# A fused decoder block on one core: attention operands stored contiguously in DRAM, queries held in half tiles

## The chip, the core and the metric

The kernel runs on one core of a Trainium2 chip, in one launch. The metric is the device time of one execution in microseconds; smaller is better. Inputs and outputs are float32.

## What is computed

One decoder layer on a sequence of 2048 tokens of width 1024, then a final norm. Cut to what matters here:

```python
h = rmsnorm(x, norm1_g)
p = h @ w_in                       # 2560 columns: pooling, q/k/v of two attentions
a = pool_mixer(p[..., :256])
b = diff_attention(...)            # 4 heads, two 64-wide softmax maps, 128-wide values
c = stick_breaking_attention(...)  # 4 heads of 64
x = x + concat(a, b, c) @ w_out
x = x + (silu(h2 @ w_gate) * (h2 @ w_up)) @ w_down     # h2 = rmsnorm(x, norm2_g)
return rmsnorm(x, final_norm_g)
# scores, both kinds: q (scaled by 1/8) . k over 64 channels, causal
```

## The kernel before

**Tiling.** The sequence is cut in `NT` = 4 tiles of `TQ` = 512 tokens. `a1_tile` (L534) does one tile of the first part: norm, transposes (`norm_transpose`, L453 to L469), and the projection in ten units of 256 columns (`UNITS[t]`, L37). `attention` (L838) goes over the same tiles and, in `ORDER[t]` (L36), over six pairs of heads: four of the differential attention (`att_diff`, L710), two of stick-breaking attention (`att_sb`, L789). Then come `out_proj` and `mlp`, which the change does not touch.

**Precision.** Matmul operands are split in a high and a low float32r part (`split`, L414: ScalarE casts at L415, VectorE subtracts at L416). Dense products take three matmuls (`mm3`, L473 to L476). A score takes two, and packs the parts in the partitions: a key tile holds the 64 channels of the high part in partitions 0 to 63 and of the low part in 64 to 127; the query operand holds the same 64 channels twice, `q[0]` with the high part, `q[1]` with the low one. So L657 gives q_high times (k_high + k_low) and L658 adds q_low times the same. L660 adds the causal mask.

**Through DRAM.** Projected queries and keys come out as 128 rows (two heads or maps `r` of 64 channels) by 512 tokens. They are split into a buffer `st` (L601 and L603 for queries), stored to `q_d` or `k_d` (L611, one store of 512 KB, high and low parts as two planes of all 2048 tokens), and loaded in the other arrangement: `load_q` (L622) makes four loads of 256 KB for a pair and tile (L626: two parts, each twice, into 64 partitions), `load_kv` (L632) two of 256 KB for a key tile (L635) and one of 512 KB or two of 256 KB for values (L640, L645). Before the scores of query tile t, a pair needs its queries of tile t and its keys and values of tiles 0 to t.

**Buffers.** SBUF is laid out in rings of slots. `q0` and `q1` have the slots w31 and w32, and a second one each, w12 and w13, which come free only when the projections' ring `wr` (same slots) has served its last weight. Keys have four slots, two more later; so do values. A slot is loaded again when its last reader is done.

**Order.** All operations are recorded with an engine, an estimated duration, buffers and a priority. `Plan.schedule` (L145) lays them out on five engines by its own estimates (`dma_ns`, `LAG`, `MORE`), and the result is the fixed order of every engine's instructions. Projections of tiles 1 to 3 have lower priority on TensorE than attention: they fill what attention leaves. All loads and stores are issued by SP, in order: one that waits for a buffer or for data holds back those behind it.

Of the kernel before, what the change touches and what calls it, by code (L numbers as in the profile page):

```python
# [19 lines left out]
P = 128  # L20
S = 2048
# [26 lines left out]
def f32(ap):  # L48
    return ap.bitcast(F32)
# [226 lines left out]
def hybrid_block_kernel(  # L276
# [24 lines left out]
    q_d = [dram.tile([2, P, S], F32, name=f"q_d{p}") for p in range(PAIRS)]  # L301
    k_d = [dram.tile([2, P, S], F32, name=f"k_d{p}") for p in range(PAIRS)]
    vd_d = [dram.tile([P, S // P, 2, P], F32, name=f"vd_d{p}") for p in range(DIFF_PAIRS)]
    vs_d = [dram.tile([P, S // P, 2, 64], F32, name=f"vs_d{p}") for p in range(2 * SB_PAIRS)]
# [229 lines left out]
    def a1_tile(pl, rg, t, prio, prio_pe, first):  # L534
# [10 lines left out]
        if t == 0:  # L545
            constants(pl, {"w": rb["q1"], "h": rb["p0"]}, prio + 0.5, xs[3:])
        late = []
        for un in UNITS[t]:
# [30 lines left out]
            for c, ps in enumerate(pend):  # L579
# [4 lines left out]
                if is_v:  # L584
# [3 lines left out]
                    for h in range(nh):  # L588
                        split(pl, lambda h=h, stv=stv: stv()[:, h, :, 0, :], lambda h=h, stv=stv: stv()[:, h, :, 1, :],
                              lambda h=h, pv=pv: pv()[:, :, h, :], TQ // nh, True, [ps], (st, (h, 0)), (st, (h, 1)),  # L590
                              prio)
                        dst = vs_d[h] if un == 9 else vd_d[2 * (un - 5) + h]
                        pr = DIFF_PAIRS + h // 2 if un == 9 else 2 * (un - 5) + h
                        blk0 = 4 * t + 2 * c
                        pl.op("dma", dma_ns(P * 4096 // nh), lambda dst=dst, blk0=blk0, h=h, stv=stv: nc.sync.dma_start(
                            dst[:, blk0:blk0 + 2, :, :], f32(stv()[:, h])), r=[(st, (h, 0)), (st, (h, 1))],
                            w=[(m_v[pr][t], (c, h))], prio=prio)
                else:
                    isq = un in (1, 2, 7)
                    if isq:  # L600
                        pl.op("act", act_ns(TQ), lambda st=st, ps=ps: nc.scalar.mul(st.t[:, 0, :], ps.t, 0.125),  # L601
                              r=[ps], w=[(st, 0)], prio=prio)
                        pl.op("dve", dve_ns(TQ), lambda st=st, ps=ps: nc.vector.scalar_tensor_tensor(  # L603
                            st.t[:, 1, :], ps.t, 0.125, f32(st.t[:, 0, :]), ALU.mult, ALU.subtract),
                            r=[ps, (st, 0)], w=[(st, 1)], prio=prio)
                    else:
                        split(pl, lambda st=st: st.t[:, 0, :], lambda st=st: st.t[:, 1, :], lambda ps=ps: ps.t,
                              TQ, True, [ps], (st, 0), (st, 1), prio)
                    pair = {1: 0, 2: 2, 7: 4, 3: 0, 4: 2, 8: 4}[un] + c
                    dst, mk = (q_d, m_q) if isq else (k_d, m_k)  # L610
                    pl.op("dma", dma_ns(P * 4096), lambda st=st, dst=dst[pair]: nc.sync.dma_start(  # L611
                        dst[:, :, t0:t0 + TQ].rearrange("l p t -> p l t"), f32(st.t)),
                        r=[st], w=[mk[pair][t]], prio=prio)
# [8 lines left out]
    def load_q(pl, rg, t, p, prio):  # L622
        q = [rg["q0"].new(), rg["q1"].new()]
        for hl in range(2):
            for dup in range(2):
                pl.op("dma", dma_ns(64 * 4096) * 1.3, lambda hl=hl, dup=dup: nc.sync.dma_start(  # L626
                    f32(q[hl].t[64 * dup:64 * dup + 64]),
                    q_d[p][hl, :, t * TQ:(t + 1) * TQ].rearrange("(r d) t -> d r t", r=2)),
                    r=[m_q[p][t]], w=[(q[hl], dup)], prio=prio)
        return q  # L630

    def load_kv(pl, rg, p, j, prio):  # L632
        k, v = rg["k"].new(), rg["v"].new()
        for hl in range(2):
            pl.op("dma", dma_ns(64 * 4096) * 1.3, lambda hl=hl: nc.sync.dma_start(  # L635
                f32(k.t[64 * hl:64 * hl + 64]),
                k_d[p][hl, :, j * TQ:(j + 1) * TQ].rearrange("(r d) t -> d r t", r=2)),
                r=[m_k[p][j]], w=[(k, hl)], prio=prio)
        if p < DIFF_PAIRS:
            pl.op("dma", dma_ns(P * 4096), lambda: nc.sync.dma_start(  # L640
                f32(v.t), vd_d[p][:, 4 * j:4 * j + 4].rearrange("p b l e -> p (b l e)")),
                r=[m_v[p][j]], w=[v], prio=prio)
        else:
            for r in range(2):
                pl.op("dma", dma_ns(P * 2048), lambda r=r: nc.sync.dma_start(  # L645
                    f32(v.t[:, r * TQ:(r + 1) * TQ]),
                    vs_d[2 * (p - DIFF_PAIRS) + r][:, 4 * j:4 * j + 4].rearrange("p b l e -> p (b l e)")),
                    r=[m_v[p][j]], w=[(v, r)], prio=prio)
        return k, v

    def scores(pl, rg, q, kt, r, g, j, t, strict, prio):
        n = TQ if j < t else (g + 1) * P
        s = rg["s"].new()
        qs = slice(g * P, (g + 1) * P)

        def qk():
            nc.tensor.matmul(s.t[:, :n], q[0].t[:, r, qs], kt.t[:, r, :n], start=True, stop=False)  # L657
            nc.tensor.matmul(s.t[:, :n], q[1].t[:, r, qs], kt.t[:, r, :n], start=False, stop=j < t)  # L658
# [3 lines left out]
        pl.op("pe", 2 * mm_ns(n) + (60 if j == t else 0), qk, r=[*q, kt], w=[s], prio=prio)  # L662
# [713 lines left out]
    def banks(ids):  # L1376
# [22 lines left out]
        q0=ring([2, TQ], F32R, ("w", [31, 12])), q1=ring([2, TQ], F32R, ("w", [32, 13])),  # L1399
# [73 lines left out]
```

## Time and profile before

| what | value |
|---|---|
| median of three runs | 2718.97 us (2711.99 to 2724.35) |
| the profiled execution | 2719.03 us, its span 2717.2 us |
| PE (TensorE matmul) busy | 2601.9 us, 96% |
| DVE, ACT, POOL busy | 1786.2 us, 1319.3 us, 870.0 us |
| share of the chain that ended last | PE 72%, DMA 9%, DVE 9% |
| loads of q_d, k_d | 96 and 120, of 256 KB |
| stores to q_d, k_d | 24 and 24, of 512 KB |

The profile is of one execution. Busy time of TensorE is the union of matmuls that overlap in its pipeline: one of 512 columns shows about 0.4 us, but the next begins 0.23 us after it. "[1.27 <-DMA d<-q_d]" behind an instruction says that its engine stood idle for 1.27 us, ended by a transfer from `q_d`. All tiles in SBUF are called `d`; lines tell them apart. [...] The first 1390 us hold projections, attention and output projection; the rest is the MLP.

### The profile page before, as it was taken

What the parts mean: (1) busy time and instruction counts of PE and PEld (TensorE: products, weight loads), DVE (VectorE), ACT (ScalarE), POOL (GpSimd) and SP (SyncE); (2) the same over time, 40 slices, a digit from 0 to 9 for tenths busy, and PEclk for the clock granted to TensorE, in tenths of its full rate; (3) what the DMA queues carried; (4) which work ended last, traced back from release to release, by engine and by line L of the source; (5) the groups of instructions that cost most, each with busy time, mean ns of one, the idle gap of its engine ahead of it and who ended that gap; (6) DMA issues with size and microseconds to landing.
All of it is one profiled execution on the core that took longest, in us unless ns stands there. A gap on an engine that the chain in (4) does not pass through costs nothing.

```text
span 2717.2 us, 39503 instructions
## 1 busy us (share of the span) xinstructions
PE 2601.9 (96%) x13836; PEld 2176.7 (80%) x13836; DVE 1786.2 (66%) x3131; ACT 1319.3 (49%) x2645; POOL 870.0 (32%) x890
## 2 busy tenths in 40 slices
PE   9989989989999999999989999999999998999998
PEld 7878778877888788888978877888888886888886
DVE  6366787758887888788656666545444447558557
ACT  4365566646666666665534444323333333445444
POOL 1001212212254124133015456535454544132041
PEclk9989999989999999999999999999999999999999
DMA  6786585556564775664534457465222338335223
GB/s 217 245 251 184 160 245 160 155 155 202 153 177 147 225 203 147 192 178 161 166 118 155 155 184 239 158 220 199 101 102 97 109 129 291 118 95 194 93 90 120
DMA packets 223480, 454.27 MB, mean 167 GB/s; under 512 B 23720, under 2 KB 70952, under 8 KB 223280
## 3 DMA queue, kind: packets, MB, share of 16 engines
q1 hardware_dynamic: 223280, 451.75, 52.9%
q8 instruction: 108, 1.77, 0.3%
q14 instruction: 92, 0.75, 0.1%
HBM read 321.11 MB, written 130.55 MB: 166 GB/s over the span
## 4 chain that ended last, share of the span: by engine, by line
PE 72%; DMA 9%; DVE 9%; issue 3%; ACT 2%; POOL 1%; SPq 1%; DVEq 0%; ACTq 0%; POOLq 0%
PE bank L474 16%; PE bank L476 16%; PE bank L475 16%; DVE d L416 4%; DMA d<-q_d 4%; PE bank L657 3%; PE bank L681 3%; PE bank L658 3%; DMA d<-wo_d 2%; PE bank L924 2%; PE bank L923 2%; PE bank L925 2%; ACT d L415 1%; PE bank L562 1%; PE bank L781 1%
## 5 line engine op out<-in xcount | busy, mean ns | idle before, releaser
L474 PE MATMUL bank<-d 128*128 128x512 f32 x2296 | 919.0, 400 | 14.0 <-DVE d L1122 9.8
L476 PE MATMUL bank<-d 128*128 128x512 f32 x2296 | 910.3, 396 | 5.7 <-DVE d L416 5.4
L416 DVE TENSOR_TENSOR d<-d 128x512 fp32r<-128x512 f32 (+2 forms) x672 | 614.6, 938 | 457.5 <-ACT d L415 281.2
L475 PE MATMUL bank<-d 128*128 128x512 f32 x2296 | 909.3, 396 | 3.4 <-DVE d L416 3.4
L415 ACT CAST d<-d 128x512 fp32r<-128x512 f32 (+2 forms) x672 | 489.0, 758 | 651.0 <-PE bank L476 352.3
L961 POOL TENSOR_TENSOR d<-d 128x512 f32<-128x512 f32 x336 | 520.0, 1556 | 846.3 <-DVE d L416 622.9
L474 PEld LDWEIGHTS bank<-d 128*128 128x128 f32 x2296 | 435.7, 190 | 116.0 <-DVE d L1122 12.4
L476 PEld LDWEIGHTS bank<-d 128*128 128x128 f32 x2296 | 434.3, 189 | 110.3 <-DVE d L416 8.7
L475 PEld LDWEIGHTS bank<-d 128*128 128x128 f32 x2296 | 434.8, 189 | 101.3 <-DVE d L416 5.1
L416 DVE TENSOR_TENSOR d<-bank,d 128x512 fp32r<-128x512 f32 (+3 forms) x381 | 219.3, 603 | 139.7 <-ACT d L415 138.7
L819 POOL TENSOR_TENSOR d<-d 128x512 f32<-128x512 f32 (+3 forms) x160 | 160.4, 1003 | 397.9 <-DVE d L815 375.6
L415 ACT CAST d<-bank 128x512 fp32r<-128x512 f32 (+3 forms) x381 | 187.5, 529 | 194.0 <-PE bank L681 122.0
L729 ACT ACTIVATE d<-bank,d 128x512 f32<-128x512 f32 (+3 forms) x320 | 198.9, 627 | 128.4 <-DVE d L726 120.3
L751 POOL TENSOR_SCALAR d<-d 128x512 f32<-128x512 f32 (+3 forms) x144 | 95.8, 681 | 448.7 <-ACT d L741 318.1
L726 DVE TENSOR_REDUCE d<-bank 128x1 f32<-128x512 f32 (+3 forms) x320 | 186.9, 602 | 61.6 <-PE bank L658 31.1
L657 PE MATMUL bank<-d 128*128 128x512 f32 (+3 forms) x480 | 203.7, 425 | 24.8 <-ACT d L729 9.0
L658 PE MATMUL bank<-d 128*128 128x512 f32 (+3 forms) x480 | 181.9, 382 | 25.5 <-DMA d<-q_d 25.5
L1122 DVE TENSOR_TENSOR d<-bank,d 128x512 f32<-128x512 f32 x176 | 121.0, 687 | 116.0 <-PE bank L476 98.7
L815 DVE TENSOR_TENSOR_SCAN d<-d,bank 128x512 f32<-128x512 f32 (+3 forms) x160 | 174.3, 1090 | 19.6 <-ACT d L807 8.1
L1118 ACT COPY d<-bank 128x512 f32<-128x512 f32 x132 | 77.3, 586 | 221.7 <-PE bank L476 196.9
L681 PE MATMUL bank<-ident,d 128*128 128x128 f32 x1088 | 157.5, 279 | 3.4 <-DVE d L772 2.6
L923 PE MATMUL bank<-d 128*128 128x256 f32 x512 | 149.5, 292 | 2.8 <-DMA d<-wo_d 1.1
(133 smaller groups left out, 3593.5 us busy)
## 6 DMA issues: line engine op xcount, KB each, us to landing
d<-in_w_gu_dram SPq DMA_DIRECT2D x88, 512.0 KB, 3.5
d<-in_w_in_dram SPq DMA_DIRECT2D x80, 512.0 KB, 4.6
d<-k_d SPq DMA_DIRECT2D x120, 256.0 KB, 6.6
d<-wo_d SPq DMA_DIRECT2D x52, 512.0 KB, 6.0
d<-q_d SPq DMA_DIRECT2D x96, 256.0 KB, 6.3
d<-vd_d SPq DMA_DIRECT2D x40, 512.0 KB, 4.9
g_d<-d SPq DMA_DIRECT2D x66, 256.0 KB, 2.1
d<-g_d SPq DMA_DIRECT2D x66, 256.0 KB, 2.7
```

The costliest lines, as they stand in the source:

```text
L415: pl.op("act", act_ns(n, psum), lambda: nc.scalar.copy(hi(), src()), r=r, w=[whi], prio=prio)
L416: pl.op("dve", dve_ns(n), lambda: nc.vector.tensor_sub(lo(), src(), f32(hi())), r=[*r, *after, whi], w=[wlo], prio=prio)
L474: nc.tensor.matmul(o, a_hi, b_hi, start=first, stop=False, **kw)
L475: nc.tensor.matmul(o, a_hi, b_lo, start=False, stop=False, **kw)
L476: nc.tensor.matmul(o, a_lo, b_hi, start=False, stop=last, **kw)
L657: nc.tensor.matmul(s.t[:, :n], q[0].t[:, r, qs], kt.t[:, r, :n], start=True, stop=False)
L658: nc.tensor.matmul(s.t[:, :n], q[1].t[:, r, qs], kt.t[:, r, :n], start=False, stop=j < t)
L681: nc.tensor.transpose(tp.t[:, c:c + P], rows[qb][kb // 4].t[:, (kb % 4) * P:(kb % 4 + 1) * P], ident)
L726: pl.op("dve", dve_ns(n), lambda s=s, n=n, mc=mc, sm=sm: nc.vector.tensor_reduce(sm.t[:, mc:mc + 1], s.t[:, :n], AX, ALU.max, negate=True) ...
L729: pl.op("act", act_ns(n, True, 2), lambda s=s, n=n, e=e, mc=mc, lc=lc, sm=sm: nc.scalar.activation(e.t[:, :n], s.t[:, :n], AF.Exp, bias=sm ...
L923: nc.tensor.matmul(o, m[:, 0, cs], wh.t[:, k % 4, :], start=k == 0, stop=False)
L961: pl.op(eng, ns, lambda: en.tensor_tensor(out(), a(), b(), op), r=r, w=w, prio=prio)
```

## The change

DRAM tensors are split by pair and tile, and laid out as the loads want them. Queries are held in halves of 256 tokens: a half tile has `[r][part][256]` in each partition, and partitions 2d and 2d + 1 both hold channel d, from one load that reads each row twice. Key parts alternate in the same way: partition 2d holds channel d of the high part, 2d + 1 of the low part. So the sum over 128 partitions is the same. Both are now one load of 512 KB, 4 KB in each partition; values of the stick-breaking pairs too. Stores of queries and keys are two of 256 KB, one for each `r`, from 64 partitions each. The four query slots form one ring of half tiles, of which two are free before `wr` ends. A score waits for its half alone.

```diff
-    q_d = [dram.tile([2, P, S], F32, name=f"q_d{p}") for p in range(PAIRS)]
-    k_d = [dram.tile([2, P, S], F32, name=f"k_d{p}") for p in range(PAIRS)]
+    q_d = [[dram.tile([2, 64, 2, 2, 256], F32, name=f"q_d{p}_{t}") for t in range(NT)] for p in range(PAIRS)]
+    k_d = [[dram.tile([64, 2, 2, TQ], F32, name=f"k_d{p}_{t}") for t in range(NT)] for p in range(PAIRS)]
+    v_d = [[dram.tile([P, D], F32, name=f"v_d{p}_{t}") for t in range(NT)] for p in range(PAIRS)]
...
-                        pl.op("act", act_ns(TQ), lambda st=st, ps=ps: nc.scalar.mul(st.t[:, 0, :], ps.t, 0.125),
+                        part = lambda l, st=st: st.t.rearrange("p h (l t) -> p h l t", l=2)[:, :, l, :]
+                        src = lambda ps=ps: ps.t.rearrange("p (h t) -> p h t", h=2)
+                        pl.op("act", act_ns(TQ), lambda part=part, src=src: nc.scalar.mul(part(0), src(), 0.125),
...
-                    pl.op("dma", dma_ns(P * 4096), lambda st=st, dst=dst[pair]: nc.sync.dma_start(
-                        dst[:, :, t0:t0 + TQ].rearrange("l p t -> p l t"), f32(st.t)),
-                        r=[st], w=[mk[pair][t]], prio=prio)
+                    for r in range(2):
+                        pl.op("dma", dma_ns(P * 2048), lambda st=st, dst=dst[pair][t], r=r, isq=isq: nc.sync.dma_start(
+                            dst[:, :, r].rearrange("h d l t -> d h (l t)") if isq else dst[:, :, r],
+                            f32(st.t[64 * r:64 * r + 64])), r=[st], w=[(mk[pair][t], r)], prio=prio)
...
     def load_q(pl, rg, t, p, prio):
-        q = [rg["q0"].new(), rg["q1"].new()]
-        for hl in range(2):
-            for dup in range(2):
-                pl.op("dma", dma_ns(64 * 4096) * 1.3, lambda hl=hl, dup=dup: nc.sync.dma_start(
-                    f32(q[hl].t[64 * dup:64 * dup + 64]),
-                    q_d[p][hl, :, t * TQ:(t + 1) * TQ].rearrange("(r d) t -> d r t", r=2)),
-                    r=[m_q[p][t]], w=[(q[hl], dup)], prio=prio)
+        q = []
+        for h in range(2):
+            qh = rg["q"].new()
+            q.append(qh)
+            pl.op("dma", dma_ns(P * 4096), lambda h=h, qh=qh: nc.sync.dma_start(
+                f32(qh.t), q_d[p][t][h].rearrange("(d o) r l t -> d o (r l t)", o=1).to_broadcast([64, 2, D])),
+                r=[m_q[p][t]], w=[qh], prio=prio)
         return q
...
-        for hl in range(2):
-            pl.op("dma", dma_ns(64 * 4096) * 1.3, lambda hl=hl: nc.sync.dma_start(
-                f32(k.t[64 * hl:64 * hl + 64]),
-                k_d[p][hl, :, j * TQ:(j + 1) * TQ].rearrange("(r d) t -> d r t", r=2)),
-                r=[m_k[p][j]], w=[(k, hl)], prio=prio)
+        pl.op("dma", dma_ns(P * 4096), lambda: nc.sync.dma_start(
+            f32(k.t), k_d[p][j].rearrange("d l r t -> (d l) r t")), r=[m_k[p][j]], w=[k], prio=prio)
...
-        qs = slice(g * P, (g + 1) * P)
+        qh, c0 = q[g // 2], 2 * r * 256 + g % 2 * P
...
-            nc.tensor.matmul(s.t[:, :n], q[0].t[:, r, qs], kt.t[:, r, :n], start=True, stop=False)
-            nc.tensor.matmul(s.t[:, :n], q[1].t[:, r, qs], kt.t[:, r, :n], start=False, stop=j < t)
+            nc.tensor.matmul(s.t[:, :n], qh.t[:, c0:c0 + P], kt.t[:, r, :n], start=True, stop=False)
+            nc.tensor.matmul(s.t[:, :n], qh.t[:, c0 + 256:c0 + 256 + P], kt.t[:, r, :n], start=False, stop=j < t)
...
-        pl.op("pe", 2 * mm_ns(n) + (60 if j == t else 0), qk, r=[*q, kt], w=[s], prio=prio)
+        pl.op("pe", 2 * mm_ns(n) + (60 if j == t else 0), qk, r=[qh, kt], w=[s], prio=prio)
...
-        q0=ring([2, TQ], F32R, ("w", [31, 12])), q1=ring([2, TQ], F32R, ("w", [32, 13])),
+        q=ring([D], F32R, ("w", [31, 32, 12, 13])),
```

Lines of the changed kernel: the query and key store is L613, the query load L630, the key load L637, the two score matmuls L648 and L649, the mask L651.

With it the planner's order changes on every engine. Three places, rows in the order of one engine.

SP, tile 1, pair 0: the key tile of tile 1 goes to DRAM and back. Before:

```order
L611 DMA k_d0_66<-d_2925 128x2x512
L635 DMA d_2959<-k_d0_66 64x2x512
L412 DMA d_2970<-in_w_in_dram 128x1024
L611 DMA k_d1_67<-d_2957 128x2x512
L412 DMA d_2987<-in_w_in_dram 128x1024
L635 DMA d_2959<-k_d0_66 64x2x512
L635 DMA d_3002<-k_d1_67 64x2x512 x2
```

Now:

```order
L613 DMA k_d0_1_85<-d_2970 128x1x512 x2
L637 DMA d_3005<-k_d0_1_85 128x1024
L412 DMA d_3018<-in_w_in_dram 128x1024
L613 DMA k_d1_1_89<-d_3003 128x1x512 x2
L412 DMA d_3043<-in_w_in_dram 128x1024
L637 DMA d_3063<-k_d1_0_88 128x1024
L637 DMA d_3083<-k_d1_1_89 128x1024
```

Before, the two loads of key tile d_2959 stand apart, with two weight loads and the next pair's store between them; now the one load of d_3005 stands right behind its two stores.

SP, tile 1, the queries of pair 2 (`q_d2`). Before:

```order
L635 DMA d_3542<-k_d3_69 64x2x512 x2
L611 DMA q_d4_64<-d_3524 128x2x512
L626 DMA d_3584<-q_d2_62 64x2x512 x2
L626 DMA d_3609<-q_d2_62 64x2x512 x2
L412 DMA d_3634<-in_w_out_dram 128x1024
L635 DMA d_3653<-k_d3_69 64x2x512 x2
```

Now:

```order
L412 DMA d_3304<-in_w_in_dram 128x1024
L630 DMA d_3372<-q_d2_1_69 128x1x1024
L639 DMA d_3420<-v_d2_0_116 128x1024
L639 DMA d_3463<-v_d2_1_117 128x1024
L698 DMA o_d1_133<-d_3448 128x512
L637 DMA d_3488<-k_d3_0_96 128x1024
L630 DMA d_3534<-q_d2_1_69 128x1x1024
```

Before, the four loads of both parts stand together, behind a key load of pair 3; now the first half (d_3372) stands ahead of pair 2's values, and the second half (d_3534) five rows later.

PE, the first score of pair 5 on tile 1, whose keys of tile 1 are projected in the last unit of `UNITS[1]`. Before:

```order
L562 MATMUL bank1_162<-d_4021,d_4051 128x256
L563 MATMUL bank1_162<-d_4040,d_4051 128x256
L564 MATMUL bank1_162<-d_4021,d_4051 128x256
L562 MATMUL bank1_162<-d_4021,d_4055 128x256
L563 MATMUL bank1_162<-d_4040,d_4055 128x256
L564 MATMUL bank1_162<-d_4021,d_4055 128x256
L657 MATMUL bank2_166<-d_4086,d_4386 128x128
L658 MATMUL bank2_166<-d_4086,d_4403 128x128
```

Now:

```order
L462 MATMUL bank0_210<-ident_163,d_1629 128x128
L462 MATMUL bank0_210<-ident_163,d_1656 128x128
L462 MATMUL bank0_210<-ident_163,d_1679 128x128
L462 MATMUL bank0_210<-ident_163,d_1702 128x128
L462 MATMUL bank1_214<-ident_163,d_1629 128x128
L462 MATMUL bank1_214<-ident_163,d_1656 128x128
L462 MATMUL bank1_214<-ident_163,d_1679 128x128
L462 MATMUL bank1_214<-ident_163,d_1702 128x128
L648 MATMUL bank2_218<-d_4420,d_4281 128x128
L649 MATMUL bank2_218<-d_4420,d_4281 128x128
```

Before, projection matmuls of a value unit (L562 to L564) stand ahead of it; now it is the transposes of the next tile's norm (L462), 28 of them and four small matmuls between the last matmul of the key unit and this score.

## Rows read from the trace of the kernel before

**Rows 1.** The page, busy time of each engine (share of the span), instructions: TensorE.

```profile
PE 2601.9 (96%) x13836; PEld 2176.7 (80%) x13836; DVE 1786.2 (66%) x3131; ACT 1319.3 (49%) x2645; POOL 870.0 (32%) x890
```

**Rows 2.** Spans and mean granted TensorE clock of the core.

```profile
core 0: 2717.2 us, clock 0.977
```

**Rows 3.** Waits (us, times, longest); then who waited for q_d, for k_d (us, times).

```profile
PE bank L658 <- DMA d<-q_d: 25.5, 14, 3.7
...
  PE bank L657: 2.0, 3
...
  PE bank L657: 6.5, 3
```

**Rows 4.** Eleven stretches after such waits: us, PE busy, granted clock, DMA share, GB/s.

```profile
199.00:207.00 8.00, 8.00 (x42) 0.57 0.65 223
...
578.00:589.00 11.00, 8.55 (x24) 0.53 0.51 175
...
885.00:890.00 5.00, 4.16 (x17) 0.66 0.39 135
sum 63.00, PE 56.01; mean PE 5.09
```

**Rows 5.** Timeline of PE: start us, us, line and operation, [idle before <-releaser].

```profile
565.80 0.39 PE L475 MATMUL bank<-d 128*128 128x512 f32 x1
566.03 0.40 PE L476 MATMUL bank<-d 128*128 128x512 f32 x1
...
580.45 0.77 PE L658 MATMUL bank<-d 128*128 128x512 f32 x1 [3.70 <-DMA d<-q_d]
...
885.84 0.77 PE L658 MATMUL bank<-d 128*128 128x512 f32 x1 [1.46 <-DMA d<-q_d]
```

**Rows 6.** Timeline of SP's queue, 566 to 572 us.

```profile
566.15 0.58 SPq L626 DMA_DIRECT2D d<-q_d  x1
...
570.66 0.33 SPq L412 DMA_DIRECT2D d<-in_w_in_dram  x1
571.09 1.24 SPq L626 DMA_DIRECT2D d<-q_d  x2
```

**Rows 7.** Lines L626 (query loads), L640 (value loads), L611 (query and key stores).

```profile
L626 SPq DMA_DIRECT2D d<-q_d x96: 573/580/1285, 38.3 to 1149.7; - x96
...
DMA to landing us min/median/max: 4.3/6.3/9.6
...
DMA to landing us min/median/max: 3.8/4.9/9.7
...
DMA to landing us min/median/max: 2.7/3.6/7.5
```

**Rows 8.** Timelines of ACT, SP and PE, 272 to 290 us: one key tile.

```profile
272.88 0.59 ACT L415 CAST d<-bank 128x512 fp32r<-128x512 f32 x1 [3.94 <-PE bank L476]
...
274.22 0.37 SPq L611 DMA_DIRECT2D k_d<-d  x1
276.99 0.58 SPq L635 DMA_DIRECT2D d<-k_d  x1
...
281.14 0.33 SPq L412 DMA_DIRECT2D d<-in_w_in_dram  x1
281.52 1.88 SPq L635 DMA_DIRECT2D d<-k_d  x3
...
289.09 0.44 PE L657 MATMUL bank<-d 128*128 128x128 f32 x1 [2.65 <-DMA d<-k_d]
```

**Rows 9.** Timeline of PE, 641 to 649 us: transposes for a projection tile.

```profile
644.41 0.66 PE L462 MATMUL bank<-ident,d 128*128 128x128 f32 x4 [0.97 <-DVE d L467]
645.66 0.66 PE L462 MATMUL bank<-ident,d 128*128 128x128 f32 x4 [0.60 <-DVE d L738]
647.18 1.11 PE L462 MATMUL bank<-ident,d 128*128 128x128 f32 x4 [0.86 <-DVE d L467]
```

**Rows 10.** One stretch: us, busy time (instructions) by engine, clock, DMA share, GB/s.

```profile
100.00:900.00 800.00, 743.90 (x4488) 640.01 (x4487) 577.25 (x1126) 478.44 (x1097) 191.52 (x306) 0.95 0.63 184
```

More of the change, by code (lines that the diff above doesn't have):

```diff
@@ L299, in hybrid_block_kernel @@
     dram = ctx.enter_context(tc.tile_pool(name="dram", bufs=1, space=bass.MemoryType.DRAM))
-    q_d = [dram.tile([2, P, S], F32, name=f"q_d{p}") for p in range(PAIRS)]
-    k_d = [dram.tile([2, P, S], F32, name=f"k_d{p}") for p in range(PAIRS)]
-    vd_d = [dram.tile([P, S // P, 2, P], F32, name=f"vd_d{p}") for p in range(DIFF_PAIRS)]
-    vs_d = [dram.tile([P, S // P, 2, 64], F32, name=f"vs_d{p}") for p in range(2 * SB_PAIRS)]
+    q_d = [[dram.tile([2, 64, 2, 2, 256], F32, name=f"q_d{p}_{t}") for t in range(NT)] for p in range(PAIRS)]
+    k_d = [[dram.tile([64, 2, 2, TQ], F32, name=f"k_d{p}_{t}") for t in range(NT)] for p in range(PAIRS)]
+    v_d = [[dram.tile([P, D], F32, name=f"v_d{p}_{t}") for t in range(NT)] for p in range(PAIRS)]
     o_d = [dram.tile([KB, P, TQ], F32, name=f"o_d{t}") for t in range(NT)]
@@ L545, in a1_tile @@
         if t == 0:
-            constants(pl, {"w": rb["q1"], "h": rb["p0"]}, prio + 0.5, xs[3:])
+            constants(pl, {"w": rb["q"], "h": rb["p0"]}, prio + 0.5, xs[3:])
         late = []
@@ L591, in a1_tile @@
                               prio)
-                        dst = vs_d[h] if un == 9 else vd_d[2 * (un - 5) + h]
                         pr = DIFF_PAIRS + h // 2 if un == 9 else 2 * (un - 5) + h
[L594 to L597, printed above, removed]
+                        o0, w = (h % 2 * TQ if un == 9 else 0) + 4 * c * e, 4 * e
+                        pl.op("dma", dma_ns(P * 4096 // nh), lambda dst=v_d[pr][t], o0=o0, w=w, h=h, stv=stv: nc.sync.dma_start(
+                            dst[:, o0:o0 + w], f32(stv()[:, h].rearrange("p b l e -> p (b l e)"))),
+                            r=[(st, (h, 0)), (st, (h, 1))], w=[(m_v[pr][t], (c, h))], prio=prio)
                 else:
@@ L600, in a1_tile @@
                     if isq:
-                        pl.op("act", act_ns(TQ), lambda st=st, ps=ps: nc.scalar.mul(st.t[:, 0, :], ps.t, 0.125),
+                        part = lambda l, st=st: st.t.rearrange("p h (l t) -> p h l t", l=2)[:, :, l, :]
+                        src = lambda ps=ps: ps.t.rearrange("p (h t) -> p h t", h=2)
+                        pl.op("act", act_ns(TQ), lambda part=part, src=src: nc.scalar.mul(part(0), src(), 0.125),
                               r=[ps], w=[(st, 0)], prio=prio)
-                        pl.op("dve", dve_ns(TQ), lambda st=st, ps=ps: nc.vector.scalar_tensor_tensor(
-                            st.t[:, 1, :], ps.t, 0.125, f32(st.t[:, 0, :]), ALU.mult, ALU.subtract),
+                        pl.op("dve", dve_ns(TQ), lambda part=part, src=src: nc.vector.scalar_tensor_tensor(
+                            part(1), src(), 0.125, f32(part(0)), ALU.mult, ALU.subtract),
                             r=[ps, (st, 0)], w=[(st, 1)], prio=prio)
@@ L633, in load_kv @@
         k, v = rg["k"].new(), rg["v"].new()
-        for hl in range(2):
-            pl.op("dma", dma_ns(64 * 4096) * 1.3, lambda hl=hl: nc.sync.dma_start(
-                f32(k.t[64 * hl:64 * hl + 64]),
-                k_d[p][hl, :, j * TQ:(j + 1) * TQ].rearrange("(r d) t -> d r t", r=2)),
-                r=[m_k[p][j]], w=[(k, hl)], prio=prio)
[L639 to L648, printed above, removed]
+        pl.op("dma", dma_ns(P * 4096), lambda: nc.sync.dma_start(
+            f32(k.t), k_d[p][j].rearrange("d l r t -> (d l) r t")), r=[m_k[p][j]], w=[k], prio=prio)
+        pl.op("dma", dma_ns(P * 4096), lambda: nc.sync.dma_start(f32(v.t), v_d[p][j]), r=[m_v[p][j]], w=[v], prio=prio)
         return k, v
```

## The prediction

> **What bounds the kernel now.** The page comes first: TensorE is busy 96% of the span [rows 1], so the kernel is bound by TensorE, and an edit that leaves the matmuls alone can only give back TensorE's idle time and the time at the lower clock. The clock view shows a mean of 0.977 [rows 2], so about 2717 x 0.023 = 62 us go there. Next the waits of TensorE, by releaser: the second score matmul (L658) waits 25.5 us, 14 times, for query loads, the first (L657) 2.0 us, 3 times; loads of keys cost 6.5 us, 3 times [rows 3]. That is 27.5 + 6.5 = 34.0 us idle. [...] Length times (1 - clock), summed over the eleven, gives 25.7 us; 56.01 of the 63 us were busy [rows 4], so 22.9 us were really lost. **All that query and key loads cost TensorE is 34.0 + 22.9 = 56.9 us, 1.67 us per microsecond waited.**
>
> Where does a wait come from? The last wait for queries ends at 885.84 us [rows 5]. Until the projections are done, ring `q0` and ring `q1` have one slot each (the second ones, w12 and w13, belong to the projections' ring `wr`), so all four query loads of a pair must wait for the last score of the pair before. Around the longest wait the first of four goes out at 566.15 us, the last two only at 571.09, behind a weight load (570.66) that was held up [rows 6]; the score that needs them starts at 580.45 [rows 5]. Between the last score on a slot and the next one there stood, counted in the order before and priced at 0.23 us per 512 columns, fewer in proportion [rows 5], only some 6.3 to 10 us of other matmuls at most boundaries.
>
> **The change, part by part.**
>
> *Half-tile query slots.* A half holds 256 of the 512 queries, both their high and low parts. Two halves fit until the projections end, and the first is free once the first half of the pair's scores is done. Counted in the same way in the new order, the TensorE work between the last score on a slot and the first score of the next load grows to 10 to 38 us for nearly all halves of tiles 1 to 3. That is above the worst landing of a query load, 9.6 us [rows 7]. So the 27.5 us and their clock go. Nine halves stay tight: 5.6, 6.0, 5.3, 5.1, 5.8 and 4.8 us in tile 0, and 6.2, 6.1, 6.1 later. The new load (128 partitions by 4 KB, one issue) is nearest to the value load of L640: 3.8 us at best, 4.9 median, 9.7 at worst [rows 7]. With 4.9 us and 1 us for a load in front that is not ready, 5.9 us against those nine gaps leaves 0.3 + 0.6 + 0.8 + 0.1 + 1.1 = 2.9 us of waiting.
>
> *One key load.* A key tile is now one load behind its stores. Before, the two loads of one tile were torn apart: the key store went out at 274.22, the first load at 276.99, the second at 281.52, since a weight load stood between them until 281.14 [rows 8]. The 6.5 us go with the 27.5.
>
> *What is late next.* With queries early, attention catches up with the projections, and TensorE meets tiles that were projected just before. Six first scores in the new order read a query or key whose last projection matmul stands only 9.4, 9.0, 3.8, 9.1, 10.4 and 9.1 us of TensorE work ahead (sum 50.8). Before, the tightest four were 12.4 to 15.5 us. The trip goes matmul, ScalarE, VectorE, store, load. From ScalarE's start to the store's issue it takes 274.22 - 272.88 = 1.34 us [rows 8], say 1.4 with the start; the second half's store adds its issue, 0.4 [rows 8]; a store lands after 3.6 us, a load after 4.9 (medians of the whole store and of the value load, the nearest shapes) [rows 7]; 1 us for the queue. **Trip: 11.3 us.** Waits: 1.9 + 2.3 + 7.5 + 2.2 + 0.9 + 2.2 = 17.0 us. The queue's 1 us is chosen between 0 (the load stands directly behind its stores in five of the six) and the 3.9 us that the torn load lost, nearer to 0 for that reason. With the best landings (2.7 and 3.8) and no queue the trip is 8.3 us, with the worst (7.5 and 9.7) 19.0 [rows 7]; between them a whole trip of before lay at 16.2 (below), and I keep 8.3 and 16.2 as ends. In the 3.8 us case only transposes stand in between, which VectorE paces too (1.25 to 1.5 us for each four) [rows 9]; the place may show as a wait for VectorE instead, at a like price.
>
> *Stores.* 48 stores of 512 KB become 96 of 256 KB from 64 partitions. On SP that is 48 x 0.37 = 18 us more [rows 8]; against it 96 + 120 + 80 loads become 48 + 60 + 60, and the old query ones took 0.58 us each [rows 7]. SP's queue gets shorter; its time is on the path only inside the trips above. The two halves use different partitions, and I let them run side by side. The key load waits at the head of SP's queue for both stores; behind it stand a weight load and the next stores, as before.
>
> [...]
>
> *Nothing or next to it.* ScalarE and VectorE write the query parts in two runs of 256; that is 48 operations on engines that are not the bound, and inside a trip they are in the 1.34 us; without that cover a tenth of a microsecond on each query trip. Matmul count and shapes are the same, as are the bytes.
>
> **Sum.** Out: 56.9. Back: (17.0 + 2.9) x 1.67 = 33.3. Net -23.6 us. The profiled execution took 2719.03 us, the median of the runs is 2718.97, so no correction: **2696 us**. With 0 to 2 us for the queue (half of what the torn load lost) it is 2681 to 2719.
>
> **The rivals.**
>
> *All cover.* With the trip of 8.3 us only the 3.8 us place waits, 4.5 x 1.67 = 7.5, net -49.4: 2670 us. For it: the load is alone on the queue in several places. Against: medians are a third higher.
>
> *The trip stays as it was, slower.* One trip of before, measured as it ran, took 289.09 - 272.88 = 16.2 us [rows 8]. If the new one does too (half stores one after the other alone make it 11.3 + 3.6 = 14.9 and the time 2731 us), the six places wait 6 x 16.2 - 50.8 = 46.4 us, with the halves 49.3 x 1.67 = 82.3: +25.4, 2744 us. It breaks even at a trip of 13.7 us. Against: 281.52 - 276.99 = 4.5 us of the 16.2 were the torn second load, which no longer exists.
>
> *The gain is eaten elsewhere.* The planner lays out every queue anew. Between 100 and 900 us TensorE idles 56.1 us [rows 10], some 22 of them not for queries or keys but for ScalarE and VectorE. If these grow by half, 11 x 1.67 = 18 us come back: 2714 us. For it: transposes that had matmuls between them now stand bare at one boundary. Against: at another, where they stood bare [rows 9], they are now covered. A change that fails to do what it says, with queries still late, would look like this too.
>
> **How the numbers follow.** A measurement of this kernel tells about 0.5%, 13.6 us, from no change. Forecast 0.53, all cover 0.20, eaten elsewhere 0.15, trip unchanged 0.12. Faster than 2705.4: all of the second and about 0.7 of the first, 0.57. Slower than 2732.6: 0.12. The rest, 0.31, lies within. The range reaches from the second case to half way between break-even and the slow one: 2668 to 2730 us.
>
> **What would show it.** Right: waits of the score matmuls for queries fall from 27.5 to below 5 us and lie mostly before 250 us; the clock between 100 and 900 us rises above 0.95 [rows 10]; new waits for key or query loads, about six, sum to about 17 us, the longest at the change from tile 1's projections to tile 2's; nothing moves behind 1400 us. Wrong: query waits that stay above 10 us with wide gaps in the order, trips far from 11.3 us, or a growth of TensorE's waits for VectorE and ScalarE.

## The result and the profile after

The changed kernel takes 2687.41 us (2686.77 to 2688.6 in four runs), the kernel before beside it 2720.24. The ratio is 0.9884, 95% interval 0.986 to 0.9907: faster by 1.2%. The forecast was 2696 us, faster, with a range of 2668 to 2730. The profiled execution took 2687.28 us, against 2719.03 before: 31.8 us less, where the sum had said 23.6.

The page of the changed kernel, busy times: TensorE is as full as before [rows 1], in a shorter span.

```profile
span 2685.5 us, 39424 instructions
...
PE 2582.1 (96%) x13836; PEld 2159.8 (80%) x13836; DVE 1785.1 (66%) x3131; ACT 1325.7 (49%) x2649; POOL 877.3 (33%) x890
```

The clocks view, to be read against [rows 2]: the mean granted clock, a share of full speed, rose from 0.977 to 0.982.

```profile
core 0: 2685.5 us, clock 0.982
```

The waits of TensorE's matmuls by releaser (us, times, longest). L648 is the first score matmul; L672 is a transpose in attention; L882 is a broadcast ahead of the output projection.

```profile
PE bank L648 <- ACT d L720: 10.3, 11, 3.9
...
PE bank L882 <- DVE d L887: 6.9, 2, 6.5
...
PE bank L648 <- DMA d<-k_d: 6.8, 3, 4.4
...
PE bank L648 <- DVE d L806: 6.5, 7, 2.3
...
PE bank L672 <- DVE d L763: 5.8, 6, 1.6
```

Who waited for the query tensor, and how long its loads took (us; the last line has issue to landing, minimum, median and maximum for stores and loads together):

```profile
  PE bank L648: 0.3, 1
...
DMA to landing us min/median/max: 3.2/4.0/7.7
```

Against [rows 3], the 27.5 us that TensorE waited for queries are down to 0.3, in one wait. The 6.5 us for keys are 6.8, but not the same ones. Before, each of the three tiles had its two loads torn apart (issued at 276.99 and 281.52 us in [rows 8], at 593.06 and 597.62, at 994.21 and 1004.55); now a tile is one load. Two of the three waits, 4.37 and 0.60 us, are for a tile that was projected just before. The third, 1.82 us, is not: that tile was stored at 567.5 us, and its load went out only at 604.95. The one query wait, 0.28 us, is at the first score of tile 1, whose queries went to DRAM at 234.13 us and were loaded from 238.12 on: a fresh tile too.

```profile
241.97 0.50 PE L648 MATMUL bank<-d 128*128 128x512 f32 x1 [0.28 <-DMA d<-q_d]
...
510.31 0.33 PE L648 MATMUL bank<-d 128*128 128x128 f32 x1 [0.60 <-DMA d<-k_d]
...
611.62 0.30 PE L648 MATMUL bank<-d 128*128 128x128 f32 x1 [1.82 <-DMA d<-k_d]
```

The query loads by their line, L630, to be read against the 6.3 us median of [rows 7]:

```profile
L630 SPq DMA_DIRECT2D d<-q_d x48: 518/546/1251, 40.0 to 1089.9; - x48
...
DMA to landing us min/median/max: 3.4/4.5/7.7
```

The key loads likewise, by L637; before, the median by L635 was 6.6 us for loads of half the bytes:

```profile
DMA to landing us min/median/max: 3.2/4.9/8.3
```

The longest of the three key waits stands where the forecast had put its longest, between projections of tile 1 and tile 2. TensorE's timeline there (start us, us, operation, idle before and its releaser):

```profile
392.93 1.32 PE L462 MATMUL bank<-ident,d 128*128 128x128 f32 x8 [1.41 <-DVE d L467]
395.15 1.97 PE L462 MATMUL bank<-ident,d 128*128 128x128 f32 x8 [0.90 <-DVE d L467]
401.49 0.45 PE L648 MATMUL bank<-d 128*128 128x128 f32 x1 [4.37 <-DMA d<-k_d]
```

SP's queue in the same stretch, the two stores of the key tile and three key loads:

```profile
390.18 1.17 SPq L613 DMA_DIRECT2D k_d<-d  x2
392.24 0.34 SPq L412 DMA_DIRECT2D d<-in_w_in_dram  x1
395.23 1.28 SPq L637 DMA_DIRECT2D d<-k_d  x3
```

ScalarE began to split that tile at 388.84 us, so this trip took 401.49 - 388.84 = 12.6 us, against 16.2 us in [rows 8]. TensorE waited for VectorE for 1.41 + 0.90 us at the transposes on the way. The DMA was crowded: between 386 and 402 us its share was 0.86, against 0.60 between 100 and 900 us, and half stores landed after 4.4 us and key loads after 6.6 us at the median, against 3.6 and 4.9 us over the whole run.

The stretches at the lower clock that touch waits for queries or keys are now two, where [rows 4] had eleven (us, PE busy, granted clock, DMA share, GB/s). In the first, slices of 0.25 us show a granted clock of 0.50 from 394.50 to 404.50 us, and 1.00 before 394.25 and behind 404.75:

```profile
394.00:405.00 11.00, 5.72 (x25) 0.53 0.58 195
612.00:617.00 5.00, 5.00 (x23) 0.66 0.67 185
```

Weighed as before, busy time times (1 - clock), these lose 5.72 x 0.47 + 5.00 x 0.34 = 4.4 us, against 22.9.

**The account.** Query and key loads cost TensorE 34.0 + 22.9 = 56.9 us before and 7.1 + 4.4 = 11.5 us after: 45.4 us less. The span fell by 31.7. So some 14 us came back. Most of it shows as waits for other engines: those for L720, L806, L763 and L887 above (10.3, 6.5, 5.8 and 6.9 us) were in the kernel before:

```profile
PE bank L657 <- ACT d L729: 9.0, 13, 2.8
...
PE bank L657 <- DVE d L815: 2.9, 8, 0.7
PE bank L681 <- DVE d L772: 2.6, 5, 0.8
...
PE bank L891 <- DVE d L896: 1.6, 2, 1.1
```

These four are 29.5 against 16.1 us, 13.4 us more. The spans and busy times close the account. TensorE's idle time, span less busy time, fell only from 2717.2 - 2601.9 = 115.3 to 2685.5 - 2582.1 = 103.4 us: 26.9 us less for queries and keys, 15.0 us more for all else. Its busy time fell by 19.8 us, the larger part of the gain, near the 22.9 - 4.4 = 18.5 us of clock above. Clock too came back elsewhere: weighed over the whole span in stretches of 1 us, the loss fell from 53.2 to 37.3 us, while between 900 and 1400 us it rose from 12.5 to 20.0.

### The profile page after: what moved, and what is told of

Its sections match the earlier page's. It is cut to its first block, busy times and chain, and to the rows that moved or that the text cites. A ratio compares the mean times of both kernels' runs of the same rounds, so it can differ in the third digit from the quotient of the medians.

```text
span 2685.5 us, 39424 instructions
## 1 busy us (share of the span) xinstructions
PE 2582.1 (96%) x13836; PEld 2159.8 (80%) x13836; DVE 1785.1 (66%) x3131; ACT 1325.7 (49%) x2649; POOL 877.3 (33%) x890
## 4 chain that ended last, share of the span: by engine, by line
PE 60%; DVE 9%; DMA 6%; ACT 3%; issue 2%; POOL 1%; SPq 1%; DVEq 0%; ACTq 0%; POOLq 0%
PE bank L474 14%; PE bank L476 14%; PE bank L475 14%; DVE d L416 4%; PE bank L672 3%; PE bank L648 2%; PE bank L649 2%; DVE d L806 2%; PE bank L915 2%; PE bank L914 2%; ACT d L415 1%; PE bank L916 1%; DMA d<-wo_d 1%; PE bank L817 1%; DMA h_d<-d 1%
## 5 line engine op out<-in xcount | busy, mean ns | idle before, releaser
L416 DVE TENSOR_TENSOR d<-bank,d 128x512 fp32r<-128x512 f32 (+4 forms) x381 | 220.0, 604 | 112.4 <-ACT d L415 108.1
L415 ACT CAST d<-bank 128x512 fp32r<-128x512 f32 (+4 forms) x381 | 187.8, 527 | 189.5 <-PE bank L672 109.2
L720 ACT ACTIVATE d<-bank,d 128x512 f32<-128x512 f32 (+3 forms) x320 | 198.5, 626 | 107.0 <-DVE d L717 102.3
L742 POOL TENSOR_SCALAR d<-d 128x512 f32<-128x512 f32 (+3 forms) x144 | 102.7, 729 | 441.0 <-ACT d L732 394.6
L648 PE MATMUL bank<-d 128*128 128x512 f32 (+3 forms) x480 | 199.9, 417 | 27.9 <-ACT d L720 10.3
L806 DVE TENSOR_TENSOR_SCAN d<-d,bank 128x512 f32<-128x512 f32 (+3 forms) x160 | 174.5, 1091 | 31.9 <-ACT d L798 14.2
L649 PE MATMUL bank<-d 128*128 128x512 f32 (+3 forms) x480 | 176.7, 371 | 0.0
L672 PE MATMUL bank<-ident,d 128*128 128x128 f32 x1088 | 156.5, 277 | 6.9 <-DVE d L763 5.8
```

The source lines that it names most:

```text
L415: pl.op("act", act_ns(n, psum), lambda: nc.scalar.copy(hi(), src()), r=r, w=[whi], prio=prio)
L416: pl.op("dve", dve_ns(n), lambda: nc.vector.tensor_sub(lo(), src(), f32(hi())), r=[*r, *after, whi], w=[wlo], prio=prio)
L648: nc.tensor.matmul(s.t[:, :n], qh.t[:, c0:c0 + P], kt.t[:, r, :n], start=True, stop=False)
L649: nc.tensor.matmul(s.t[:, :n], qh.t[:, c0 + 256:c0 + 256 + P], kt.t[:, r, :n], start=False, stop=j < t)
L672: nc.tensor.transpose(tp.t[:, c:c + P], rows[qb][kb // 4].t[:, (kb % 4) * P:(kb % 4 + 1) * P], ident)
L720: pl.op("act", act_ns(n, True, 2), lambda s=s, n=n, e=e, mc=mc, lc=lc, sm=sm: nc.scalar.activation(e.t[:, :n], s.t[:, :n], AF.Exp, bias=sm ...
```

## Experiments

Three theories were on record. **A**, the slots: a half can be loaded while the other half still works, so loads start early. **B**, the transport: one wide load instead of two or four narrow ones lands earlier and can't be torn. **C**, the order: the planner laid out everything anew, and that is worth the gain. Ratios are to the kernel before on the same chip, with 95% intervals.

### Half tiles with the old kind of load

Query halves as in the change, each loaded by two loads of 64 partitions; keys and values as before.

```diff
...
+            for dup in range(2):
+                pl.op("dma", dma_ns(64 * 4096) * 1.3, lambda h=h, qh=qh, dup=dup: nc.sync.dma_start(
+                    f32(qh.t[64 * dup:64 * dup + 64]), q_d[p][t][h].rearrange("d r l t -> d (r l t)")),
...
```

> Half tiles alone: each half is loaded by two loads of 256 KB into 64 partitions, keys and values as before. Theory A (the slots: loads start half a pair earlier): waits of the score matmuls for queries fall from 27.5 us to below 5, time 2690 to 2702. Theory B (the transport: fewer, wider loads land earlier): waits for queries stay above 15 us, time 2708 to 2722. Theory C (the new order of all engines, not the transfers): query waits fall little, and other waits of TensorE fall instead.

Measured: 2708.51 us, ratio 0.9949 (0.9933 to 0.9966). TensorE waited 5.0 us for queries, but for keys:

```profile
  PE bank L666: 16.2, 8
```

Query waits fall as A says, the time by less than A said, since key waits rise from 6.5 to 16.2 us. Of these, 7.9 us are for tiles stored 11 to 15 us earlier: attention meets fresh keys sooner, three of the four times with two torn loads. The other 8.3 us are for tiles stored more than 60 us earlier, whose loads went out late; why, no run shows.

### The layout with whole tiles

All of the change but the halves: each query part is one load of 512 KB in alternating copies, one slot each.

```diff
-        q=ring([D], F32R, ("w", [31, 32, 12, 13])),
+        q0=ring([2, TQ], F32R, ("w", [31, 12])), q1=ring([2, TQ], F32R, ("w", [32, 13])),
```

> The layout alone: keys and values as in the change, queries in whole tiles, one slot for each part until the projections end, each part one load of 512 KB in alternating copies. Theory A (slots): query waits stay, 15 us or more, since a load still starts only after the last score of the pair before; time 2705 to 2720. Theory B (transport): the load lands 3 to 4 us earlier, inside the 6.3 to 10 us of other matmuls at a boundary, query waits fall below 6 us, time 2688 to 2700. Theory C: as for the other run, the waits that move are not those for queries.

Measured: 2700.92 us, ratio 0.9919 (0.9896 to 0.9941). The waits for queries:

```profile
  PE bank L649: 7.8, 9
  PE bank L648: 1.6, 3
```

Keys cost 4.5 us. With the slots of before, query waits fall from 27.5 to 9.4 us. That is between A's 15 and B's 6, and the time lies between the two ranges, 0.9 us above B's. So **both parts work**: 0.81% for the transport and 0.51% for the slots alone, 1.2% together. Which of them is worth more is not settled: the two intervals overlap, and this run has the wide key loads while the other kept the torn ones. Waits for queries alone fell further with the slots (5.0 us) than with the transport (9.4 us). The wide value loads were not tried alone; TensorE shows no wait for a value load, before or after.

### A second query slot, all else as before

```diff
-        q0=ring([2, TQ], F32R, ("w", [31, 12])), q1=ring([2, TQ], F32R, ("w", [32, 13])),
+        q0=ring([2, TQ], F32R, ("w", [31, 26])), q1=ring([2, TQ], F32R, ("w", [32, 30])),
```

Keys and values give up one slot each (w26, w30) and get w12 and w13 later.

> The kernel before, transfers and layout untouched, with a second slot for each query part from the start, taken from keys and values (three slots each until the projections end, four before). Theory A (slots): query waits fall from 27.5 us to below 5; waits for keys may appear on tile 2, where a pair needs three; time 2690 to 2712. Theory B (transport): query waits stay above 12 us, since four torn loads land as late as before; time 2710 or more.

Measured: 2717.78 us, ratio 0.9974 (0.9954 to 0.9994), slower than the 2690 to 2712 us that A allowed and inside B's 2710 or more. The waits, though, went A's way. Those for the query tensor:

```profile
  PE bank L658: 0.2, 1
```

Those for the key tensor:

```profile
  PE bank L657: 33.4, 18
```

A second slot alone removes the query waits whole (0.2 of 27.5 us are left), with transfers that land as late as before (5.9 us at the median for stores and loads of queries together, before 5.8). A's mechanism is shown. But key waits of 33.4 us took back what was won. Some 11.5 us of them are at tiles stored less than 16 us earlier, as in the first experiment. The other 21.9 us, thirteen waits, are for tiles stored long before, whose loads went out only 6 to 12 us ahead of the score. That the third slot less held them back is likely, but not shown apart from the new order. Halves give the head start without more room, and that is their point.

### Copies that do not alternate

The change with the two copies in the lower and upper 64 partitions, key parts likewise, still single loads.

```diff
-                f32(qh.t), q_d[p][t][h].rearrange("(d o) r l t -> d o (r l t)", o=1).to_broadcast([64, 2, D])),
+                f32(qh.t), q_d[p][t][h].rearrange("(o d) r l t -> o d (r l t)", o=1).to_broadcast([2, 64, D])),
...
-            f32(k.t), k_d[p][j].rearrange("d l r t -> (d l) r t")), r=[m_k[p][j]], w=[k], prio=prio)
+            f32(k.t.rearrange("p r t -> p (r t)")), k_d[p][j].rearrange("d l r t -> l d (r t)")), r=[m_k[p][j]], w=[k], prio=prio)
```

> The change with the two copies of a query row in the lower and the upper 64 partitions, and key parts likewise, in single loads of the same size and the same order of instructions. Theories A and B alike: no difference from the change, within 4 us of it (2687), query landing median 4.0 us within 0.5; if alternation itself mattered, landing medians would rise by over 1 us and the time by over 8 us.

Measured: 3362.69 us, ratio 1.2348 (1.232 to 1.2376). A and B missed by 675 us; only the last clause, over 8 us if alternation itself matters, went the right way. The DMA view by stretches around one query load (us, PE busy, clock, DMA share, GB/s) shows why:

```profile
306.00:308.00 2.00, 2.00 (x20) 1.00 0.66 255
...
310.00:312.00 2.00, 2.00 (x18) 1.00 0.13 53
312.00:314.00 2.00, 2.00 (x18) 1.00 0.13 53
```

While only such loads are under way, the DMA engines are busy for a share of 0.13 and move 53 GB/s: as much as two of sixteen engines would be if always busy (0.13 x 16 = 2.1, an estimate from that share). The source of a query load is a pattern of 2 by 64 by 1024, in the change 64 by 2 by 1024; the tile it fills has 128 partitions in both. Why that order matters, no run shows. TensorE then waited, for keys and queries:

```profile
PE bank L648 <- DMA d<-k_d: 180.2, 17, 23.1
PE bank L648 <- DMA d<-q_d: 166.8, 22, 16.4
```

So in this kernel alternation is what lets one load fill 128 partitions with two copies of 64 rows in 4.5 us, its median in the change. Two loads of 64 partitions would do that too; the next run is that.

### The wide loads split in two

Each query half and key tile by two loads of 256 KB into 64 partitions, 4 KB rows as in the change. The run was made twice, with the planner's estimate of a load plain, and then raised by the factor 1.3 of the kernel before.

```diff
...
+        for hl in range(2):
+            pl.op("dma", dma_ns(P * 2048), lambda hl=hl: nc.sync.dma_start(
+                f32(k.t[64 * hl:64 * hl + 64]), k_d[p][j][:, hl]), r=[m_k[p][j]], w=[(k, hl)], prio=prio)
```

> The change with every query half and every key tile loaded by two loads of 256 KB into 64 partitions each (lower and upper half, no alternation), rows of 4 KB as in the change. Theory: it is the single wide load, not the 4 KB rows, that lands early and keeps a tile from being torn: query and key landing medians rise from 4.0 and 4.4 us towards 5, the time to 2692 to 2702. Rival: the contiguous rows are what counts, and splitting costs under 4 us: 2684 to 2691.

> The run split_wide_loads again, with the planner's estimate of each split load raised by the factor 1.3 that the kernel before uses. If the split lost because the planner took it for as quick as the wide load, key waits fall from some 17 us to 8 to 12 and the ratio to 0.991 to 0.995; if the split transfers themselves cost the gain, the ratio stays at 0.997 or above.

Measured: 2724.36 us, ratio 0.999 (0.9976 to 1.0005), and 2724.82, ratio 1.0001 (0.9984 to 1.0017). The whole gain is gone. Both ranges of the first expectation were missed (2692 to 2702, 2684 to 2691), and the planner's estimate is not the cause. The first run waited 4.0 us for queries and 19.6 for keys. In the second run the key loads, to be read against L637 above:

```profile
L639 SPq DMA_DIRECT2D d<-k_d x120: 444/588/1209, 89.9 to 1162.1; - x120
...
DMA to landing us min/median/max: 3.4/5.7/9.6
```

Who waited for the key tensor there:

```profile
  PE bank L650: 15.0, 6
```

Queries cost another 8.7 us, so 23.7 against 7.1 us in the change. There are twice the issues, for keys at 0.59 us instead of 0.33, and a median of 5.7 instead of 4.9 us for half the bytes. So the single wide load carries the gain, not the 4 KB rows; the run with whole key stores below says the same, as its loads gather rows of 2 KB and lose nothing. By its waits for queries and keys this kernel should be near the first experiment (21.2 us, ratio 0.9949), and is not. The traces show where part of the rest went: TensorE's idle time is 130.2 us against 121.2 there, with busy times alike (2592.6 and 2592.0). Waits for ScalarE are 25.8 against 18.7 us, and 6.9 against 3.4 us have no releaser that the profile shows. Why these grew stays open.

### The same kernel in another order

The kernel before with only the planner's estimate of query and key loads changed.

```diff
-                pl.op("dma", dma_ns(64 * 4096) * 1.3, lambda hl=hl, dup=dup: nc.sync.dma_start(
+                pl.op("dma", dma_ns(64 * 4096), lambda hl=hl, dup=dup: nc.sync.dma_start(
...
```

> The kernel before with nothing changed but the planner's own estimate of the query and key loads (its factor of 1.3 is gone): the same instructions and transfers in another order. Theory C (a new order is worth what was gained): the time may move by 15 us or more either way. Theories A and B: query waits stay above 18 us and the time within 10 us of before (2710 to 2730).

Measured: 2758.93 us, ratio 1.0122 (1.0104 to 1.014): 34 us slower with the same instructions. Waits for queries:

```profile
  PE bank L658: 41.6, 18
...
  PE bank L657: 11.0, 7
```

That is 52.6 us, and 9.1 for keys. A and B were wrong about its size; C was right that order alone moves the time by more than 15 us. But it does so through the very waits that the change removes: TensorE's idle time grew by 30.9 us (115.3 to 146.2), 27.7 of them for queries and keys. That a planner which takes a load for 0.2 us quicker puts the first score closer behind it fits this, but was not counted in the order.

The opposite, the kernel before with a later landing planned:

```diff
-"dma": (950.0, 950.0)}
+"dma": (1700.0, 1700.0)}
```

> The kernel before, transfers and slots untouched, with the planner told that a transfer's data is usable 750 ns later (as in the run longer_landing_planned). If the loss was mostly the planner's too early expectation, query waits fall from 27.5 us to 12 to 18 and the time by 12 to 22 us (ratio 0.992 to 0.996), so that part of the change's gain is had by order alone; if slots and transport bound it, the waits only turn into other waits, ratio 0.997 to 1.003.

Measured: 2707.08 us, ratio 0.9933 (0.9912 to 0.9953). As the first case expected, waits for queries fell to 14.8 us (0.4 of them at L657); those for keys were 7.9:

```profile
PE bank L658 <- DMA d<-q_d: 14.4, 13, 2.1
...
PE bank L657 <- DMA d<-k_d: 7.9, 3, 4.9
```

**About half of the gain is to be had without touching a transfer**, 20.6 us of the 40.2 that the change is worth on that chip. In its profile the idle time hardly fell, to 113.0 from 115.3 us, since waits for VectorE rose from 42.6 to 51.2; the busy time fell, from 2601.9 to 2593.5 us. So fewer waits for transfers became other waits, as the second case expected, and yet the kernel is faster.

### Stores, and the rest of the key waits

The change with the later landing planned (same edit as above):

> The change, with the planner told that a transfer's data is usable 750 ns later, so that it lays more work between store, load and first score. If the fresh key loads are what is left of transfers, TensorE's waits for keys fall from 6.8 us to below 2 and the time to 2676 to 2685; if the order matters otherwise, it lands anywhere within 10 us of 2687 with no tie to those waits.

Measured: 2688.01 us, ratio 0.9856 (0.9838 to 0.9873). The change with keys stored whole, contiguous from 128 partitions, while each partition's load gathers two rows of 2 KB:

```diff
+                        pl.op("dma", dma_ns(P * 4096), lambda st=st, dst=dst[pair][t]: nc.sync.dma_start(
+                            dst.rearrange("r d l t -> (r d) l t"), f32(st.t)), r=[st], w=[mk[pair][t]], prio=prio)
...
+            f32(k.t), k_d[p][j].rearrange("r d l t -> (d l) r t")), r=[m_k[p][j]], w=[k], prio=prio)
```

> The change with keys stored whole again (one contiguous store of 512 KB from 128 partitions, and the load gathers two rows of 2 KB for each partition). If the halved stores cost something, fresh key waits fall from 6.8 us and the time by 2 to 8 us (2679 to 2685); if the halves run side by side, no difference beyond 4 us either way.

Measured: 2687.63 us, ratio 0.9857 (0.9839 to 0.9876). Neither can be told from the change, which gave 0.9884 and, run again, 0.9857 (below). In the first, key waits are down to 0.4 us as expected, but the time missed its 2676 to 2685. TensorE was busy for 773 of the 800 us between 100 and 900 (761 in the change). The idle time of the whole run was 95.2 us against 103.4, but the busy time 2592.3 against 2582.1: what was saved in waits was lost in busy time, and why is not shown. With whole key stores, key waits are 6.2 us: halved key stores cost nothing that shows, and contiguous rows on the load's side matter little. Both edits together, and the change beside them:

> The change with whole key stores and the longer landing in the planner together, as the candidate to beat the change. If the two ratios (0.9857 and 0.9856) were both real gains on the change's 0.9884, together 0.982 to 0.985; if they are the same as the change on that chip, 0.985 to 0.989 and within 0.2% of the change run beside it.

> The change itself beside the three others on one chip, as their yardstick: ratio 0.985 to 0.990, query waits below 1 us, key waits 5 to 8 us.

Measured: 2682.97 us (2680.29 to 2684.85), ratio 0.9842 (0.9821 to 0.9863), and the change 2687.51 us (2685.5 to 2694.09), ratio 0.9857 (0.9833 to 0.9881). The runs do not overlap, the intervals do: 4.5 us or 0.17%, the best version that was found, by a step at the edge of what can be told. The ratio lies in the range for two real gains, the distance within the 0.2% for none; so the two cases are not told apart. The change beside them came as expected, with waits of 0.2 us for queries and 7.6 for keys.

### Waits and times side by side

Waits of the score matmuls for queries and keys in the profiled execution, all its idle time (span less busy time), and the median against that of before on the same chip (us):

| kernel | queries | keys | all idle time | time |
|---|---|---|---|---|
| before | 27.5 | 6.5 | 115.3 | 0 |
| the change | 0.3 | 6.8 | 103.4 | -32.8 |
| the change, run again | 0.2 | 7.6 | 106.4 | -40.2 |
| layout, whole tiles | 9.4 | 4.5 | 106.6 | -23.1 |
| half tiles, old loads | 5.0 | 16.2 | 121.2 | -15.5 |
| before, longer landing planned | 14.8 | 7.9 | 113.0 | -20.6 |
| second slot | 0.2 | 33.4 | 124.3 | -6.3 |
| split loads, first run | 4.0 | 19.6 | 130.0 | -0.7 |
| split loads, second run | 8.7 | 15.0 | 130.2 | -2.9 |
| before, replanned | 52.6 | 9.1 | 146.2 | +33.9 |
| change, longer landing planned | 0 | 0.4 | 95.2 | -37.0 |
| change, whole key stores | 0.4 | 6.2 | 107.3 | -37.4 |
| change, both edits | 0 | 0.4 | 92.8 | -44.7 |
| copies that do not alternate | 166.8 | 180.2 | 658.5 | +638.7 |

Against the 34.0 us of before, time follows the sum of the two waits in many rows: 27.7 us more of them cost 33.9, 26.9 fewer gave 32.8, 33.6 fewer gave 44.7. In seven of the thirteen rows a microsecond of waiting goes with 1.10 to 1.36 us of time. The others do not fit. The change run again has 1.5, before with the longer landing 1.8, and the copies that do not alternate 2.0. The second slot gained 6.3 us though its waits sum to 33.6, and the split loads gained 0.7 and 2.9 where some 10 us fewer waits promised four times that or more. The column of all idle time shows that the two waits are not the whole account: with half tiles, the second slot and the split loads it rose, because other waits grew by more than those for queries and keys fell. The change itself gave 32.8 and 40.2 us in two series of runs with nearly the same waits, so single profiles and single medians limit what the table can tell.

## Why the prediction was right, and where not

- **What bounds it, and where the waits come from: right.** Query waits were to vanish on nearly all halves and did, 27.5 to 0.3 us, the one that is left before 250 us as forecast. The granted clock between 100 and 900 us rose from 0.95 to 0.98, also as forecast. The second-slot run shows the cause that was named, one slot until the projections end.
- **The tight halves: too high.** The sum had 2.9 us for nine of them; none showed, since the one query wait is at a fresh tile. A half was taken to land after 4.9 us plus 1; its median is 4.5.
- **Fresh tiles: right in kind and place, too high in size.** Named as what is late next, with the longest at the change from tile 1's projections to tile 2's. It is there, 4.37 us and 2.31 us for VectorE, against 7.5 predicted. But instead of 17.0 us at six places, TensorE waited 0.28 + 4.37 + 0.60 = 5.3 us at three; with the late load at 611.62 us all waits for queries and keys are 7.1. **This is the term that was mis-sized.** The trip of 11.3 us was put together from medians over the whole run and laid on all six places. Where TensorE waited, it took 9.2 us (from ScalarE's start at 232.79 us to 241.97), 9.7 us (500.62 to 510.31) and, at the crowded place, 12.6. At two more fresh key tiles it was so short that TensorE did not wait: at most 8.8 us (below) and 8.9 us (559.77 to 568.69), near the best-case end of 8.3. With the clock, 33.3 us were put back and 11.5 measured, late load included.

The quiet trip, the first key tile of tile 1. ScalarE begins to split it at 265.12 us:

```profile
265.12 0.59 ACT L415 CAST d<-bank 128x512 fp32r<-128x512 f32 x1 [3.91 <-PE bank L476]
```

The timeline of SP's queue then has its stores and its load:

```profile
266.45 1.16 SPq L613 DMA_DIRECT2D k_d<-d  x2
270.36 0.33 SPq L637 DMA_DIRECT2D d<-k_d  x1
```

TensorE's timeline has the score that reads it, with no idle time ahead:

```profile
273.88 0.33 PE L648 MATMUL bank<-d 128*128 128x128 f32 x1
```

The load goes out behind its two stores with nothing in between, where before a weight load stood.

- **The gain is eaten elsewhere: came true in its waits.** This rival supposed 11 us more of waiting for ScalarE and VectorE, 18 us with the clock, at a chance of 0.15, and the sum had nothing for it. These waits grew from 59.1 to 76.6 us over the whole run, and their growth was also named as a sign of being wrong. The two errors are of opposite sign (21.8 us too pessimistic, some 14 too optimistic). That they nearly cancel, so that 2696 lay within 9 us, was luck. The sum itself gives 2695.4, not 2696.
- **The price of a wait, 1.67 us each, held where it was applied.** Weighed in the same way, the waits left in the changed kernel cost 11.5 / 7.1 = 1.62 us each. Between kernels a microsecond of them was worth less, 1.10 to 1.36 us of time in seven rows of the table, since part of what was saved came back elsewhere.
- **Halved stores: right to let them run side by side.** Whole key stores changed the key waits by 0.6 us and the time not measurably, and the stores' median was 3.6 us before and after.
- **What was not seen at all:** the size of order's part. The prediction counted gaps in the new order, but did not ask how much the old order could win by expecting its transfers later. By that run it can win about half.

## What to carry to other kernels

Where a planner fixes the order, compare the landing that it expects with the one in the trace: a wait that comes again at the same kind of boundary can be such a difference, and correcting the estimate is an edit of one number. It is worth a run, not a promise: here it gave 20.6 us in the kernel before and nothing that can be told in the changed one. Then look for the slot that makes the load late, and split the tile so that the first half comes free early; that needs no more room. When a load is rearranged, look at the DMA share and GB/s while it alone is under way: here the order of dimensions in the source of two loads made the kernel 23% slower, more than any other edit.

## What the runs showed of the hardware

- A 512 KB load whose source pattern began with a dimension of 2 ran at a DMA share of 0.13 and 53 GB/s; with 64 first, the same bytes landed in 4.5 us at the median.
- SP's time for an issue depends on the shape: in the changed kernel 0.33 us for 128 rows of 4 KB (key load) and 0.55 us when each row is read twice (query load); with split loads 0.55 to 0.59 us for 64 partitions. Twice the bytes for one issue was cheaper than two halves in each of these cases.
- One microsecond of TensorE's waiting for queries and keys went with 1.10 to 1.36 us of time in seven of thirteen rows of the table; matmuls behind some waits ran at a granted clock of 0.50, in the changed kernel from 394.50 to 404.50 us, where it waited 0.90 us for VectorE and 4.37 us for keys.
